# Long and short matmuls take turns on one piece of weights in a two-layer hybrid block

## The chip, the cores and the metric

One core of a Trainium2 chip runs the whole program. The metric is device microseconds of one execution. Engines: TensorE (PE; PEld is its row of weight loads), VectorE (DVE), ScalarE (ACT), GpSimd (POOL) and SyncE (SP), which issues most DMAs. TensorE's clock has two levels, 1.2 and 2.4 GHz; the profile gives the granted share.

## The reference, cut to what matters

Two layers act on 512 latent tokens and 256 context tokens of width 2048, all in float32.

```python
for l in range(2):
    sh, sc, g = split(silu(c) @ w_mod[l] + b_mod[l], 3)        # one set for latents, one for context
    hl, hc = xl * (1 + sc_l) + sh_l, xc * (1 + sc_c) + sh_c
    parts_l = split(hl @ w_in[l])       # conv u,b,c,g | q,k,v,gate | pool u,g
    parts_c = split(hc @ w_in[l])       # in the last layer only k and v
    att = softmax(q1 k1) - lam * softmax(q2 k2), applied to v   # 8 heads, keys of context and latents
    out = concat([short_conv, rms(att) * silu(gate), pool]) @ w_out[l]
    xl = layernorm(ALPHA * xl + g * out)   # and xc likewise, but in the last layer
```

What the change touches is the product `h @ w_in` for all columns but v, for both kinds of tokens at once.

## The kernel before, in words

**Numbers.** Each float32 operand is held as two halves, high and low, in a format that TensorE takes at full width (`F32R`). A product is three matmuls that accumulate in PSUM: high x high, high x low, low x high (`mm3`). The latents lie as `hhl[k]` (high) and `hll[k]` (low), 128 features by 512 tokens for each of 16 pieces k; the context as `hhc[k]` and `hlc[k]`, 128 by 256, in the tiles `hc`.

**Weights.** `WStream` brings pieces of 128 x 512 from HBM (SyncE's queue, tile `raw`), ScalarE copies the high half (`wh`, L174) and VectorE subtracts to get the low one (`wl`), up to four pieces ahead. `W.get()` hands out the next piece, `W.done()` frees its buffers for a later split.

**Stages.** A startup computes modulation and the first feature-major products; then v is made with tokens on the partitions (`v_phase`); then comes the stage of this case, 44 feature-major tiles for each layer (`mtile`); then the output product and layernorm (`gemm2`).

**`mtile`.** One call makes 128 output features for all tokens. The weights are the stationary operand (128 x 128), the tokens move past them. The sum of the latents, 512 columns, is built in one of two PSUM buffers `lat`, that of the context, 256 columns, in one of two `cps`. The loop runs over s = 0 to 7; each repetition covers two pieces k of the 16. Context tokens take part in all 44 tiles of layer 0 and in the 8 tiles of K in layer 1, 52 tiles in all; in the other 36 only the latents' matmuls run.

**Order.** All engines work through their own instruction streams, whose order the program fixes (`tc.manual_schedule()`). Attention of a head is a generator: each `step(att)` issues its next few matmuls, exponentials, transposes or subtractions between the matmuls of the tiles. With context one step stands inside a repetition (two if two heads are open) and one in `pump()` at its end. `pump` also runs work that was put off by `later` (rotary, splits of Q and K) and modulation work that is let in by a running comparison of planned VectorE and TensorE time. At s == 7 `evac` queues the copies that empty both PSUM sums, before the repetition's `pump`.

Each `PE.matmul` is recorded in the profile under the line of the wrapper that counts planned time (L53), so its rows are told apart by tiles: `lat<-hhl,wh` moves the high half of the latents past the high half of the weights, `cps<-hc,wl` the context past the low half.

Of the kernel before, what the change touches and what calls it, by code (L numbers as in the profile page):

```python
# [17 lines left out]
P = 128  # L18
D = 2048
KT = D // P  # L20
# [57 lines left out]
def body(tc, A, out):  # L78
    nc = tc.nc
    V, PE = Timed(nc.vector, dve_cost), Timed(nc.tensor, pe_cost)  # L80
    S, G, SP = nc.scalar, nc.gpsimd, nc.sync

    with tc.tile_pool(name="sb", bufs=1) as sb, tc.tile_pool(
# [115 lines left out]
        att = deque()  # L199
        modq = deque()  # L200

        def step(q):
            while q:
                try:
                    next(q[0])
                    return True
                except StopIteration:
                    q.popleft()
            return False
# [11 lines left out]
        def pump(n=1):  # L221
            for _ in range(n):
                slotn[0] += 1
                for fn in due.pop(slotn[0], ()):
                    fn()
                step(att)

                V.t = max(V.t, PE.t - LAG)
                credit[0] = min(credit[0] + rate[0], 3.0)
                if modq and credit[0] >= 1 and V.t < PE.t - left[0]:  # L230
                    credit[0] -= 1
                    step(modq)
# [62 lines left out]
        for l in range(2):  # L295
# [5 lines left out]
            for ch in range(4):  # L301
# [3 lines left out]
                for n_, k_ in enumerate(so):  # L305
                    wseq.append(A["wo"][l, ch, k_])
                    if l and n_ % 2 and (ch, n_ // 2) in SIDE:
                        extra.add(len(wseq))
                        i = SIDE.index((ch, n_ // 2))
# [13 lines left out]
        def mm3(o, hi, lo, rhi, rlo, first, last):  # L323
            PE.matmul(o, lhsT=hi, rhs=rhi, start=first, stop=False)
            PE.matmul(o, lhsT=hi, rhs=rlo, start=False, stop=False)
            PE.matmul(o, lhsT=lo, rhs=rhi, start=False, stop=last)
# [417 lines left out]
        def mtile(l, m, ctx, hook=None):  # L744
            lb[0] += 1
            pl = lat[lb[0] % 2]
            pc = cps[lb[0] % 2][:, 0:C]
            for s in range(8):
                if s % 2 == 0:
                    wh, wl = W.get()  # L750
                for hs, ps in ((hl_, pl), (hc_, pc))[:2 if ctx else 1]:
                    if hs is hc_:
                        step(att)
                        if len(att) > 1:
                            step(att)
                    for kk in range(2):
                        if not ctx and kk and len(att) > 1:
                            step(att)
                        k = 2 * s + kk
                        c = slice((k % 4) * P, (k % 4) * P + P)  # L760
                        mm3(ps, wh[:, c], wl[:, c], hs[0][k], hs[1][k], k == 0, k == KT - 1)
                if s % 2:
                    W.done()
                if s == 7:
                    evac(l, m, pl, pc)
                if hook:
                    hook(s)
                pump()

        hl_ = (hhl, hll)  # L770
        hc_ = (hhc, hlc)
# [202 lines left out]
        def evac(l, m, pl, pc):  # L974
            if M_Q <= m < M_K:
                ev_q(l, m - M_Q, pl, pc)
            elif M_K <= m < M_AG:
                ev_k(l, m - M_K, pl, pc)
            else:
                ev_x(l, m, pl, pc)  # L980
# [230 lines left out]
        for l in range(2):  # L1211
            ctx = l == 0
# [11 lines left out]
            else:  # L1224

                for k in range(KT):
                    step(hq)
                    wh, wl = W.get()
                    for i in range(4):
                        c = slice(i * P, i * P + P)  # L1230
# [30 lines left out]
            for c in lt[l]:  # L1261
                for m in c:
                    isk = M_K <= m < M_AG
                    mtile(l, m, ctx or isk, ylh if m == lt[l][-1][-1] else None)
# [79 lines left out]
```

## Time and profile before

| | |
|---|---|
| median of 3 runs | 2425.74 us (2421.2 to 2425.74) |
| the profiled execution's own time | 2427.58 us |
| its span, first to last instruction | 2425.8 us |
| TensorE busy / its loads of weights | 98% / 84% of the span |
| VectorE, ScalarE, GpSimd busy | 70%, 38%, 5% |
| mean granted clock of TensorE | 0.994 |

Busy times of TensorE come from ends that are modelled: matmuls overlap, and one that is recorded with 398 ns may be followed by the next after less. Starts are observed. A share of the whole span mixes stages, so the rows below are taken from the stage of `mtile` where that matters.

### The profile page before, as it was taken

The numbers are of one execution on the slowest core, as the hardware profiler recorded it, in microseconds if no ns is written. First come the engines' busy times: TensorE is split into PE (matmuls) and PEld (weight loads), VectorE is DVE, ScalarE is ACT, GpSimd is POOL, SyncE is SP. The second block draws the span as 40 slices with busy tenths as digits, with TensorE's granted clock in tenths as the row PEclk, the third lists the DMA queues.
The fourth block names the chain that finished last, engine by engine and source line by source line (L and its number), as shares of the span: only waits on it lengthen the run. The fifth ranks groups of instructions, "written<-read, shape, count | busy, mean of one in ns | idle before, by whom it ended". The sixth has DMA issues, their size and how long they took to land. (4 is left out here: it accounts for less than half of the span.)

```text
span 2425.8 us, 33840 instructions
## 1 busy us (share of the span) xinstructions
PE 2382.0 (98%) x12501; PEld 2032.9 (84%) x12501; DVE 1694.6 (70%) x3268; ACT 925.9 (38%) x1676; POOL 123.1 (5%) x199
## 2 busy tenths in 40 slices
PE   8999999999999999999999999999999999999997
PEld 7887888888888888888878778888888888888886
DVE  8894777787777778765486663246777677666666
ACT  4552434344343434433211153134444444444330
POOL 0000000000000000001100000000000000001102
PEclk9999999999999999999999999999999999999998
DMA  9886634343443434334456542353444434433653
GB/s 339 314 298 201 211 113 119 104 128 99 131 112 109 122 108 130 94 97 154 159 163 185 158 139 81 113 174 110 125 129 117 124 108 132 126 88 118 203 156 139
DMA packets 182169, 353.65 MB, mean 146 GB/s; under 512 B 19217, under 2 KB 43937, under 8 KB 181234
## 3 DMA queue, kind: packets, MB, share of 16 engines
q1 hardware_dynamic: 144946, 293.88, 38.8%
q0 software_dynamic: 36912, 57.55, 8.5%
q8 instruction: 98, 1.61, 0.3%
q14 instruction: 69, 0.57, 0.1%
q10 hardware_dynamic: 144, 0.05, 0.0%
HBM read 319.89 MB, written 31.51 MB: 145 GB/s over the span
## 5 line engine op out<-in xcount | busy, mean ns | idle before, releaser
L53 DVE TENSOR_TENSOR wl<-raw,wh 128x512 fp32r<-128x512 f32 x566 | 383.4, 688 | 347.8 <-ACT wh L174 346.7
L53 PE MATMUL lat<-hhl,wh 128*128 128x512 f32 x1472 | 585.6, 398 | 2.6 <-DVE Q L53 2.6
L174 ACT CAST wh<-raw 128x512 fp32r<-128x512 f32 x566 | 346.1, 619 | 614.3 <-PE SS L53 297.6
L53 PE MATMUL lat<-hll,wh 128*128 128x512 f32 x1472 | 576.6, 392 | 0.1
L53 PE MATMUL lat<-hhl,wl 128*128 128x512 f32 x1472 | 575.3, 391 | 0.0
L53 PEld LDWEIGHTS lat<-hhl,wl 128*128 128x128 f32 x1472 | 276.8, 188 | 59.6
L53 PE MATMUL cps<-hc,wh 128*128 128x256 f32 x1664 | 317.6, 284 | 0.2 <-ACT o L687 0.2
L53 PEld LDWEIGHTS lat<-hhl,wh 128*128 128x128 f32 x1472 | 277.3, 188 | 43.5 <-DVE Q L53 3.0
L53 PEld LDWEIGHTS lat<-hll,wh 128*128 128x128 f32 x1472 | 277.8, 189 | 39.7 <-DVE hll L53 0.4
L53 PEld LDWEIGHTS cps<-hc,wh 128*128 128x128 f32 x1664 | 276.7, 189 | 26.0 <-ACT o L687 0.6
L631 ACT ACTIVATE pp<-SS,smt 128x768 f32<-128x768 f32 (+1 forms) x160 | 130.9, 818 | 381.5 <-DVE smt L53 373.1
L53 PE MATMUL cps<-hc,wl 128*128 128x256 f32 x832 | 233.3, 280 | 0.0
L53 DVE CUSTOM_DVE_ANT_0 jk<-m,acc 128x512 bf16<-128x512 f32 x224 | 166.8, 745 | 19.1 <-DMA m<-in_wmbg_dram 15.2
L53 PE MATMUL SS<-wh,hc 128*128 128x512 f32 x512 | 171.1, 392 | 1.7 <-DVE aT L53 1.2
L53 PEld LDWEIGHTS cps<-hc,wl 128*128 128x128 f32 x832 | 158.9, 191 | 0.0
L53 PE MATMUL lat<-wl,hhl 128*128 128x512 f32 x364 | 144.3, 396 | 8.7 <-DVE wl L53 8.6
L53 PE MATMUL lat<-wh,hhl 128*128 128x512 f32 x364 | 145.7, 400 | 0.5 <-DVE o L53 0.5
L53 PE MATMUL lat<-wh,hll 128*128 128x512 f32 x364 | 143.6, 394 | 0.0
L53 DVE TENSOR_REDUCE smt<-SS 128x1 f32<-128x768 f32 (+1 forms) x160 | 134.9, 844 | 8.3 <-PE SS L53 7.8
L53 DVE CUSTOM_DVE_ANT_0 pp<-cv,acc 128x512 bf16<-128x512 f32 x112 | 79.8, 747 | 54.2 <-DMA cv<-in_wmbg_dram 39.3
L53 PEld LDWEIGHTS SS<-wh,hc 128*128 128x128 f32 x512 | 96.5, 188 | 24.9 <-DVE aT L53 2.1
L53 PE MATMUL SS<-K,Q 128*128 128x256 f32 (+1 forms) x432 | 109.4, 331 | 0.7 <-DVE aT L53 0.7
(269 smaller groups left out, 3552.1 us busy)
## 6 DMA issues: line engine op xcount, KB each, us to landing
raw<-in_wa_dram SPq DMA_DIRECT2D x352, 256.0 KB, 2.7
m<-in_wmbg_dram SPq DMA_DIRECT2D x200, 256.0 KB, 2.7
raw<-in_wo_dram SPq DMA_DIRECT2D x128, 256.0 KB, 3.1
wb<-in_wm0b_dram SPq DMA_DIRECT2D x32, 704.0 KB, 6.9
raw<-in_wv_dram SPq DMA_DIRECT2D x64, 256.0 KB, 3.3
cv<-in_wmbg_dram SPq DMA_DIRECT2D x56, 256.0 KB, 2.8
cv<-in_xT_dram SPq DMA_DIRECT2D x32, 384.0 KB, 4.9
v<-vsc POOLq DMA_DIRECT2D x32, 384.0 KB, 6.4
```

The source lines that it names most:

```text
L53: return fn(*a, **k)
L174: S.copy(out=h, in_=r)
L631: S.activation(out=po, in_=sv, func=AF.Exp, bias=sm[:, i:i + 1], scale=1.0, accum_out=sm[:, 2 + i:3 + i])
```

## The change

In `mtile` the two loops change places. Before, one repetition runs the latents' three matmuls for both pieces k, then attention's step, then the context's three for both pieces. After, for each piece k the three products (weights high x tokens high, high x low, low x high) are the outer loop and latents and context the inner one, so that a matmul of 512 columns and one of 256 follow each other on the same 128 x 128 piece of weights. Attention's step then stands between the two pieces k. Tiles without context keep their order.

```diff
             for s in range(8):
                 if s % 2 == 0:
                     wh, wl = W.get()
-                for hs, ps in ((hl_, pl), (hc_, pc))[:2 if ctx else 1]:
-                    if hs is hc_:
+                for kk in range(2):
+                    if kk and ctx:
                         step(att)
-                        if len(att) > 1:
-                            step(att)
-                    for kk in range(2):
-                        if not ctx and kk and len(att) > 1:
-                            step(att)
-                        k = 2 * s + kk
-                        c = slice((k % 4) * P, (k % 4) * P + P)
-                        mm3(ps, wh[:, c], wl[:, c], hs[0][k], hs[1][k], k == 0, k == KT - 1)
+                    if kk and len(att) > 1:
+                        step(att)
+                    k = 2 * s + kk
+                    c = slice((k % 4) * P, (k % 4) * P + P)
+                    first, last = k == 0, k == KT - 1
+
+                    for j, (w, i) in enumerate(((wh, 0), (wh, 1), (wl, 0))):
+                        for hs, ps in ((hl_, pl), (hc_, pc))[:2 if ctx else 1]:
+                            PE.matmul(ps, lhsT=w[:, c], rhs=hs[i][k], start=first and j == 0, stop=last and j == 2)
                 if s % 2:
                     W.done()
                 if s == 7:
```

## Rows read from the trace of the kernel before

**Rows 1.** The page: its span, and busy time of each engine.
```profile
span 2425.8 us, 33840 instructions
PE 2382.0 (98%) x12501; PEld 2032.9 (84%) x12501; DVE 1694.6 (70%) x3268; ACT 925.9 (38%) x1676; POOL 123.1 (5%) x199
```

**Rows 2.** Busy time by stage: window, length, engines' busy us, then granted clock, DMA share.
```profile
258.00:1129.00 871.00, 865.09 (x5150) 763.36 (x5149) 665.86 (x1396) 344.48 (x656) 28.92 (x44) 1.00 0.42 120
...
1594.00:2231.00 637.00, 636.00 (x3267) 541.10 (x3266) 440.48 (x781) 286.10 (x503) 25.75 (x39) 1.00 0.43 123
```

**Rows 3.** TensorE's waits, 258 to 1129 us: total, times, longest.
```profile
PE SS L53 <- ACT pp L631: 2.3, 4, 0.9
PE cps L53 <- DVE aT L53: 1.8, 2, 0.9
PE cps L53 <- DVE o L53: 1.0, 1, 1.0
```

**Rows 4.** The page's costliest groups: count, busy us, mean ns, idle before.
```profile
L53 PE MATMUL cps<-hc,wh 128*128 128x256 f32 x1664 | 317.6, 284 | 0.2 <-ACT o L687 0.2
...
L53 PEld LDWEIGHTS lat<-hll,wh 128*128 128x128 f32 x1472 | 277.8, 189 | 39.7 <-DVE hll L53 0.4
L53 PEld LDWEIGHTS cps<-hc,wh 128*128 128x128 f32 x1664 | 276.7, 189 | 26.0 <-ACT o L687 0.6
...
L53 PE MATMUL cps<-hc,wl 128*128 128x256 f32 x832 | 233.3, 280 | 0.0
```

**Rows 5.** Timeline of TensorE in layer 1, no attention: start, duration, what.
```profile
1604.45 0.39 PE L53 MATMUL lat<-hhl,wh 128*128 128x512 f32 x1
...
1605.81 0.40 PE L53 MATMUL cps<-hc,wh 128*128 128x256 f32 x2
1606.04 0.28 PE L53 MATMUL cps<-hc,wl 128*128 128x256 f32 x1
...
1606.39 0.28 PE L53 MATMUL cps<-hc,wl 128*128 128x256 f32 x1
1606.51 0.39 PE L53 MATMUL lat<-hhl,wh 128*128 128x512 f32 x1
...
1607.87 0.40 PE L53 MATMUL cps<-hc,wh 128*128 128x256 f32 x2
1608.11 0.28 PE L53 MATMUL cps<-hc,wl 128*128 128x256 f32 x1
...
1620.98 0.39 PE L53 MATMUL lat<-hhl,wh 128*128 128x512 f32 x1
```

**Rows 6.** Timeline of TensorE in layer 0, one repetition after a disturbance.
```profile
701.35 0.39 PE L53 MATMUL lat<-hhl,wh 128*128 128x512 f32 x1
...
702.04 0.39 PE L53 MATMUL lat<-hhl,wh 128*128 128x512 f32 x1
...
703.43 0.39 PE L53 MATMUL lat<-hhl,wh 128*128 128x512 f32 x1
```

**Rows 7.** Timeline of TensorE, the short matmuls of one score.
```profile
306.83 0.28 PE L53 MATMUL SS<-K,Q 128*128 128x256 f32 x1
306.94 0.28 PE L53 MATMUL SS<-v,Q 128*128 128x256 f32 x1
307.06 0.40 PE L53 MATMUL cps<-hc,wh 128*128 128x256 f32 x2
```

**Rows 8.** Timeline of TensorE, attention's product with v.
```profile
341.22 2.31 PE L53 MATMUL cps<-aT,v 128*128 128x256 f32 x18
343.37 0.41 PE L53 MATMUL cps<-hc,wh 128*128 128x256 f32 x2
```

**Rows 9.** Timeline of ScalarE at the end of a tile of K, layer 0.
```profile
291.44 0.59 ACT L819 COPY rq<-lat 128x512 f32<-128x512 f32 x1 [2.97 <-PE lat L53]
292.10 0.37 ACT L819 COPY rq<-cps 128x256 f32<-128x256 f32 x1
```

## The prediction

> **What bounds the kernel now.** I read the page first: the profiled execution spans 2425.8 us and TensorE is busy for 98% of it, VectorE for 70%, ScalarE for 38% [rows 1]. That busy time is modelled, so it says only that TensorE is the suspect. Then busy time by stage: in the feature-major products of layer 0 (258 to 1129 us) TensorE covers 865 of 871 us and in those of layer 1 (1594 to 2231 us) 636 of 637 us, at a granted clock of 1.00, the upper of its two levels, 2.4 GHz [rows 2]. Then the waits of TensorE in the longer stage: the three longest kinds sum to 2.3 + 1.8 + 1.0 = 5.1 us [rows 3]. So in both stages the queue of matmuls sets the end. A gain has to come out of the spacing of matmuls, not out of a wait.
>
> For spacing, the duration in the grouped rows (398 ns, 284 ns) is of no use, since matmuls overlap; I take start to start from the timeline. In a stretch of layer 1 without attention, eight repetitions of the loop over s (each two pieces of k: six matmuls of 512 columns and six of 256) run from 1604.45 to 1620.98 us: 16.53 / 8 = 2.066 us each, or 0.3444 us for one long and one short matmul [rows 5]. Within the first repetition the six long ones take 1605.81 - 1604.45 = 1.36 us, 0.227 each, and the six short ones 1606.51 - 1605.81 = 0.70 us, 0.117 each.
>
> **The change, part by part.** No matmul is added or removed. The edit covers 1664 + 832 = 2496 short matmuls and as many long ones (52 tiles of 48) [rows 4]. It changes three things.
>
> *Loads of weights.* The profile has one load for each matmul: 1664 loads for 1664 short matmuls of the high part. A repeat of the same piece is loaded again today: the long matmul with the low half of the latents comes right behind the one with the high half, on the same weights, and has its own 1472 loads [rows 4]. So I cost "the same piece twice in a row" at no load saved.
>
> *Spacing.* Today there are five long-to-long, one long-to-short, five short-to-short and one short-to-long step in twelve; afterwards six long-to-short and six short-to-long. The trace has both kinds. A long one followed by a short one: 1605.81 follows the last long one by the same 0.227. A short one followed by a long one: 1606.39 to 1606.51, 0.12. What the trace lacks is a short one with long ones on both sides, so this is bounded. The nearest row is the first of the short run, which has a long one before it: two short spacings in 1606.04 - 1605.81 = 0.23 us and 1608.11 - 1607.87 = 0.24 us, so 0.1175 [rows 5]. The low bound is the spacing of a score's two short matmuls behind two long ones, all four on one piece of Q: 306.83 to 306.94, about 0.1135 (half of 0.227 too), while the next, on new weights, takes 306.94 to 307.06, 0.12 [rows 7]. The high bound is attention's run on v: 18 in 343.37 - 341.22 = 2.15 us, 0.1194 each [rows 8]. I take 0.118, nearest to the rows of this very loop. A pair then costs 0.227 + 0.118 = 0.345 us against 0.3444: 0.0006 x 2496 = +1.5 us. With the low bound it is 0.0039 x 2496 = 9.7 us less, with the high one 0.0020 x 2496 = 5.0 us more.
>
> A second spacing also occurs in the loop: after some disturbances three long ones follow the short run at 0.23, from 701.35 to 702.04 (0.69 / 3), and that repetition takes 2.08 us instead of 2.066 [rows 6]. If such stretches vanished everywhere the most to win is 0.014 x 416 = 5.8 us; I take a third, 2 us less. If instead every long one behind a short one took about 0.232, the loss is 0.005 x 2496 = 12.5 us. That is the upper end.
>
> *Order around it.* Attention's step moves from behind six long ones to behind three long and three short: its two steps now stand 1.03 us apart each, where they stood 1.36 and 0.70. The number of steps, and every ScalarE, VectorE and queue instruction, stays in its order, as do the DMAs, whose issues hang on pieces of weights being split and freed. A step to the next-but-one is 2.07 us as before. Odd distances gain or lose 0.33 us; TensorE's whole wait for attention is the few us of rows 3, so I put zero there, with 3 us either way as the bound, about the 4.1 us of its two longest rows.
>
> The last long matmul of a tile now starts only 0.345 us before the tile's end instead of 0.70 + 0.227. So the copy of the latents' sum, which ScalarE was standing ready for (291.44 us, 0.59 us long, 2.97 us of idle time before it), starts 0.58 us later, and the context's copy, which ran at 292.10, queues behind it: the pair ends some 0.5 us later [rows 9]. Queued behind them on ScalarE are the split of the next weights and attention's exponentials. What hides it: the next tile uses the other PSUM buffer, a later step consumes the copies one to four repetitions on, and ScalarE is busy for only 344 of 871 us [rows 2]. Where that cover is gone, at the end of layer 0, TensorE already waits 1.0 us for VectorE's gate [rows 3]: I add 0.5 us. Uncovered for all 52 tiles it would be 26 us, which the near-absence of waits makes unlikely.
>
> Sum: +1.5 - 2 + 0.5 = 0.0 us on the profiled execution's own 2427.58 us (1.8 us more than its span). The runs shown have a median of 2425.74, 1.84 below that execution, so I state 2426.
>
> **A rule against this reading.** The rows say that a repeated piece is loaded again and that a long matmul is spaced 0.227 whether or not its weights repeat [rows 4, 5]. The Trainium skill (TensorE: Matmul & The Clock Gate, Part 2, step 1) says that weights are loaded apart from the matmul so that one load can serve several. By that the second load of each pair would be saved; the 1472 repeated loads disagree. The same page (Part 1, "Wait — 56ns, not 53.3ns?") gives 215.7 ns between 512-column matmuls at the upper clock; if missing loads brought the long ones there, the sum would be 2496 x 0.011 = 28 us less, 2398, as an estimate from that page. No run here shows it.
>
> **The rivals.** *Faster, the short matmul stops waiting for a load.* If the load of one piece can be skipped or run ahead because the piece repeats, each short spacing falls to 0.1135: for it speak the four score matmuls on one Q [rows 7]; against it, that the first two of the short run share their weights as well and take 0.1175 [rows 5]. Worked out: 2426 - 9.7 - 1.5 = 2415. Chance 0.17.
>
> *Slower, the long one behind a short one keeps the upset spacing.* Place: every short-to-long step, now 2496 instead of 416. For it: rows 6, where exactly the long ones behind a short run are late. Against: rows 5, where they aren't. At 0.232 each it gives 2426 + 12.5 = 2438. It decides from 0.002 us per pair on (4.9 us). Chance 0.16.
>
> *Slower, the late copies.* ScalarE's half microsecond per tile reaches TensorE through the exponentials; it takes more than ten of the 52 tiles exposed to show. Half of them: 2426 + 13 = 2439. Against it speaks the idle time ahead of those copies. Chance 0.05.
>
> *No effect at all*, since spacing depends only on the columns of the matmul in front: that is the forecast, 0.62.
>
> **How the numbers follow.** A difference of 0.2% (4.9 us) is about what a measurement of this kernel can tell from none. The likeliest case holds 2421 to 2431; the first rival lies about 2415, the other two about 2438. With the bounds of the short spacing and the run-to-run spread (2421.2 to 2425.74) the range is 2414 to 2439. Faster 0.17, same 0.62, slower 0.16 + 0.05 = 0.21.
>
> **What will show it.** Counts first: 1664 and 832 short matmuls, each with its load; fewer loads would make the first rival. In a stretch without attention a repetition should read 2.06 to 2.08 us, alternating 0.227 and 0.118. A repetition of 2.04 says first rival, 2.10 second. TensorE's waits in the first stage should stay below 10 us; more, on the scores or the transposes, says late copies. I am wrong if the alternation of operands and PSUM banks at every matmul has a price of its own, of which the trace before shows nothing.

## The result, and the profile after

| | before | after |
|---|---|---|
| median of 5 runs each, us | 2424.0 (2421.2 to 2425.74) | 2449.83 (2445.29 to 2450.7) |
| ratio, 95% interval | | 1.01 [1.0086, 1.0114] |
| span of the profiled execution, us | 2425.8 | 2448.0 |

The change costs 1.0%, 24 us (20.9 to 27.6 by the interval). The forecast was no change, 2426, with 2439 as the upper end. All figures below in "us against before" are the ratio less one, times 2425, with the interval worked out in the same way, so that runs of different chips can be set side by side.

Where the loss lies is seen first from busy time by stage, with the window moved to the same matmuls in each kernel: from the stage's first long matmul to the first matmul that follows its tiles (that of attention's normalization in layer 0, that of the output product in layer 1). Window, length, busy us of TensorE, its loads, VectorE, ScalarE and GpSimd, then granted clock and DMA. Of the kernel before:

```profile
257.12:1128.47 871.35, 865.44 (x5151) 763.76 (x5151) 665.87 (x1397) 344.26 (x656) 28.92 (x44) 1.00 0.42 120
1593.57:2232.96 639.39, 637.84 (x3275) 542.35 (x3273) 441.59 (x784) 287.68 (x506) 25.85 (x40) 1.00 0.43 123
```

Of the kernel after:

```profile
257.13:1149.16 892.03, 877.41 (x5150) 770.88 (x5150) 665.55 (x1397) 340.86 (x656) 28.68 (x44) 1.00 0.41 118
1613.37:2256.01 642.64, 639.75 (x3275) 543.43 (x3273) 441.42 (x784) 286.85 (x506) 25.60 (x40) 1.00 0.42 123
```

Layer 0, where 44 tiles have context, is 20.7 us longer, layer 1, where 8 have, 3.3 us; the rest of the program is not longer. The clock is the same. In layer 0 TensorE's busy time rises by 12.0 us, so 20.7 - 12.0 = 8.7 us are idle time on top: two kinds of loss, one in spacing and one in waits.

Spacing, from the timeline of the kernel after in a stretch without attention (start, duration, what):

```profile
270.31 0.40 PE L53 MATMUL lat<-hhl,wh 128*128 128x512 f32 x1
270.55 0.28 PE L53 MATMUL cps<-hc,wh 128*128 128x256 f32 x1
270.67 0.39 PE L53 MATMUL lat<-hll,wh 128*128 128x512 f32 x1
270.90 0.28 PE L53 MATMUL cps<-hc,wh 128*128 128x256 f32 x1
271.01 0.40 PE L53 MATMUL lat<-hhl,wl 128*128 128x512 f32 x1
...
271.71 0.40 PE L53 MATMUL lat<-hll,wh 128*128 128x512 f32 x1
```

Against [rows 5]: short ones still take 0.12 (270.55 to 270.67, 270.90 to 271.01), long ones take 0.24 and 0.23 by turns (270.31 to 270.55, 270.67 to 270.90), and the pattern repeats every two pairs: 271.01 - 270.31 = 271.71 - 271.01 = 0.70 us, 0.350 a pair instead of 0.3444.

That is a clean stretch. Over the whole stage of layer 0 (from 264 us on, starts of all matmuls of the loop that have matmuls of the loop on both sides, waits left out) a pair takes 345.7 ns before in the mean and 350.3 after, a long matmul 228.5 and 232.6. The kernel before has upset stretches too: a fifth of its long spacings are over 231 ns, against half after. The difference of 4.6 ns makes 11.5 us for 2496 pairs.

Waits of TensorE in the stage of layer 0 (total, times, longest), after:

```profile
PE cps L53 <- DVE aT L53: 4.1, 2, 2.1
PE SS L53 <- ACT pp L631: 3.9, 5, 1.4
PE cps L53 <- ACT o L687: 3.3, 4, 1.2
...
PE SS L53 <- DVE aT L53: 1.7, 1, 1.7
```

Against [rows 3] the wait for attention's weights aT has gone from 1.8 to 4.1 us and the one for the exponentials (pp) from 2.3 to 3.9; the third row is all but new. It says exactly what waits: the context's sum (`cps`) waits for ScalarE's o, that is, the first short matmul of a tile waits until ScalarE has read attention's product out of the other half of the same PSUM buffer (a copy, then its square, L687). It was 0.2 us before:

```profile
PE cps L53 <- ACT o L687: 0.2, 1, 0.2
```

And ScalarE at the end of a tile of K, after:

```profile
292.50 0.59 ACT L820 COPY rq<-lat 128x512 f32<-128x512 f32 x1 [3.86 <-PE lat L53]
292.98 0.38 ACT L820 COPY rq<-cps 128x256 f32<-128x256 f32 x1
293.24 0.63 ACT L174 CAST wh<-raw 128x512 fp32r<-128x512 f32 x1
```

The idle time ahead of the copy is 3.86 us instead of 2.97 [rows 9]: the copy of the latents' sum waits longer for TensorE, and what is queued on ScalarE behind it, or on VectorE for its result, can be late with it.

### The profile page after: what moved, and what is told of

It is laid out like the page before. It is cut to its first block, busy times and chain, and to the rows that moved or that the text cites. A ratio compares the mean times of both kernels' runs of the same rounds, so it can differ in the third digit from the quotient of the medians.

```text
span 2448.0 us, 33840 instructions
## 1 busy us (share of the span) xinstructions
PE 2393.7 (98%) x12501; PEld 2039.2 (83%) x12501; DVE 1694.6 (69%) x3268; ACT 921.5 (38%) x1676; POOL 122.5 (5%) x199
## 4 chain that ended last, share of the span: by engine, by line
PE 61%; DVE 6%; DMA 4%; issue 2%; ACT 1%; DVEq 0%; SPq 0%; ACTq 0%
PE lat L53 37%; PE cps L53 13%; PE SS L53 11%; DMA cv<-in_wmbg_dram 3%; DVE pp L53 2%; DVE wl L53 1%; DVE z L53 1%; DMA cv<-srow 1%; DVE bst L53 0%; DMA raw<-in_wo_dram 0%; DVE smt L53 0%; DMA m<-in_wmbg_dram 0%; DVE o L53 0%; DVE jk L53 0%; ACT wh L174 0%
## 5 line engine op out<-in xcount | busy, mean ns | idle before, releaser
L53 PE MATMUL lat<-hhl,wh 128*128 128x512 f32 x1472 | 594.0, 404 | 2.1 <-DVE Q L53 2.1
L53 PE MATMUL cps<-hc,wh 128*128 128x256 f32 x1664 | 467.8, 281 | 4.3 <-ACT o L687 4.3
L53 PEld LDWEIGHTS cps<-hc,wh 128*128 128x128 f32 x1664 | 316.7, 190 | 8.2 <-ACT o L687 6.2
```

What stands on the lines that cost most here:

```text
L53: return fn(*a, **k)
```

## The experiments

The theory after the result: three losses. (a) Spacing: a long matmul behind a single short one is spaced 6 ns more in the mean. (b) The last long matmul of a tile is late, and with it ScalarE's and VectorE's copies and attention. (c) The first short matmul of a tile is early and meets the copy out of its PSUM buffer. The rival: all is spacing.

**First repetition in the old order.** `if ctx and s == 0:` the loop of before, `else:` the new one.

> Only the first repetition (s = 0) of each tile with context runs in the old order: six long matmuls, attention's step, six short ones; the other seven take turns. Theory A (about half of the loss is waits, and the largest new one is the first short matmul of a tile, which now stands 0.23 us behind the tile's start instead of 1.36 us and waits for ScalarE's copy of attention's product out of the same PSUM buffer): that wait, 4.3 us in all after the change, goes back to 0.2, the time falls by 4 to 7 us to about 2444, one eighth of the spacing loss (1.3 us) among it. Rival B (all of the loss is spacing): only 2 to 3 us less, an eighth of 25.

Measured: 2442.89, ratio 1.0071 [1.0059, 1.0084], 17.2 us against before, so about 7 us less than after. The wait of cps on ScalarE's copy fell from 3.3 to 0.6 us in the stage of layer 0, the one on aT stayed (4.2). Loss (c) is there.

**Attention's step later.**

```diff
-                    if kk and ctx:
-                        step(att)
 ...
                     for j, (w, i) in enumerate(((wh, 0), (wh, 1), (wl, 0))):
+                        if kk and ctx and j == 1:
+                            step(att)
 ...
```

> The matmuls take turns as after the change, but attention's step stands behind the fourth of the six pairs (1.38 us into a repetition, as the 1.36 us of before) instead of the third. Theory A with waits from the moved step: the waits of attention's transposes, scores and products on ScalarE and VectorE (12 us after, 6.7 before) fall by 3 to 5 us and the time with them. Rival B (spacing alone), and the rival that the new waits come from the late copies: no change beyond 2 us.

Measured: 2447.18, 1.0086 [1.0072, 1.01], 20.9 us. Its interval overlaps that of after, so the moved step is not shown to cost; 3 us is the most likely size. The waits on aT (4.1 in the whole span) and on the copy (4.2) stayed, so neither comes from the step's place in the middle of a repetition alone.

**Last repetition in the old order.** As the first run, with `s == 7`.

> Only the last repetition (s = 7) of each tile with context runs in the old order, so that the latents' sum is complete 0.7 us before the tile's end again and ScalarE's copies start as early as before. Theory C (late copies carry the waits): 5 to 8 us less than after the change. Theories A and B: one eighth of the spacing loss, 1.3 to 3 us less.

Measured: 2438.4, 1.0051 [1.0037, 1.0065], 12.4 us, so 12 us less than after, more than expected. In the stage of layer 0 the wait on aT is back at 1.7 us, on pp at 2.3, on the copy at 1.9.

**The last, and the first, repetition alone in the new order**, all else as before (`if not (ctx and s == 7):` the old loop; and the same with `s == 0`).

> The kernel before, with only the last repetition (s = 7) of each tile with context in the new order. Theory C (the latents' sum is complete 0.58 us later, so ScalarE's and VectorE's copies, and all that is queued behind them, are late): 6 to 11 us more than before, 2431 to 2436, and more waits of TensorE on ScalarE and VectorE. Spacing alone: one eighth of 10 us, 1 to 2 us more.

> The kernel before, with only the first repetition (s = 0) of each tile with context in the new order, so that the first short matmul of a tile stands 0.23 us behind the tile's start instead of 1.36. If it then waits for the copy of attention's product out of the same PSUM buffer, TensorE shows some 4 us of waits on ScalarE's copies out of cps and the time is 4 to 7 us above before, 2430 to 2433. If that wait only arose because ScalarE was late from the tile's end, little shows: 2425 to 2428.

Measured: the last alone 2433.48, 1.0035 [1.0022, 1.0048], 8.5 us; the first alone 2429.9, 1.0017 [1.0008, 1.0027], 4.1 us. Waits of TensorE in the stage of layer 0, last repetition alone:

```profile
PE SS L53 <- ACT pp L631: 5.0, 5, 2.1
PE cps L53 <- DVE aT L53: 4.2, 2, 2.1
...
PE cps L53 <- ACT o L687: 0.6, 1, 0.6
```

First repetition alone:

```profile
PE SS L53 <- ACT pp L631: 2.0, 4, 0.8
PE cps L53 <- ACT o L687: 1.9, 3, 0.8
PE cps L53 <- DVE aT L53: 1.7, 2, 0.8
```

Each part brings its own kind of wait and hardly the other's: the late end of the long ones brings those on pp and aT, the early first short one that on the copy: 1.9 us, and 2.9 in the whole span, where some 4 were expected. The pp rows compare less well: the longest wait of the last alone stands at 318 us, soon behind the start of the stage, and from 257 to 265 us the granted clock was 1.00 in that run and 0.79 in the profile of before.

The wait on aT is the sharpest sign. In all runs whose last repetition has the old order it is 1.6 to 1.8 us, in all whose last repetition takes turns 4.1 to 4.2, and its two places in the program are the same ones at which the kernel before waits. How it grows can be followed at the first of them, in timelines of the three engines. Before:

```profile
567.78 0.82 PE L53 MATMUL SS<-ident,pp 128*128 128x128 f32 x6
567.99 0.60 ACT L800 ACTIVATE rq<-lat 128x512 f32<-128x512 f32 x1 [1.42 <-PE lat L53]
568.62 0.75 DVE L53 STREAM_SHUFFLE cv<-rq 128x512 f32<-128x512 f32 x1
573.67 0.95 DVE L53 TENSOR_TENSOR aT<-SS,aT 128x768 fp32r<-128x768 f32 x1
574.67 1.57 PE L53 MATMUL cps<-aT,v 128*128 128x256 f32 x11 [0.89 <-DVE aT L53]
```

Last repetition alone in the new order:

```profile
566.99 0.82 PE L53 MATMUL SS<-ident,pp 128*128 128x128 f32 x6
568.76 0.60 ACT L814 ACTIVATE rq<-lat 128x512 f32<-128x512 f32 x1 [2.68 <-PE lat L53]
569.40 0.75 DVE L53 STREAM_SHUFFLE cv<-rq 128x512 f32<-128x512 f32 x1
574.45 0.95 DVE L53 TENSOR_TENSOR aT<-SS,aT 128x768 fp32r<-128x768 f32 x1
575.46 1.82 PE L53 MATMUL cps<-aT,v 128*128 128x256 f32 x7 [2.11 <-DVE aT L53]
```

In this last repetition attention's step issues six transposes (first row). Before, they stand behind all six long matmuls; now they stand in front of the last three. The last long matmul starts 568.34 - 565.95 = 2.39 us into the repetition, before 567.55 - 566.42 = 1.13: 1.26 us later, where it is 0.60 us later in last repetitions without matmuls of a step. A step's matmuls lie in the last repetition of 11 of the 44 tiles of layer 0; in eight of them the last long one is 1.26 to 1.34 us later. The copy rq starts 1.77 us behind the transposes instead of 0.21. VectorE's rotary work begins with that copy, and the subtraction that completes aT is queued on VectorE 5.05 us behind the rotary's start in both. TensorE waits 2.11 us instead of 0.89. The delay went through VectorE's queue; no exponential of ScalarE lies on this path. For the waits put down to pp the path was not followed.

**Both ends old, turns between** (`s in (0, 7)` in the old order).

> First and last repetition of each tile with context in the old order, the six between take turns as after the change. If the three parts add, what is left is six eighths of the spacing loss of about 10 us: 2432 to 2435, with TensorE's waits as before. If the waits came back without the early first short matmul and the late last long one, they belong to taking turns itself: 2437 or more.

Measured: 2430.88, 1.0029 [1.0018, 1.0039], 7.0 us. Waits in the same stage:

```profile
PE cps L53 <- DVE aT L53: 1.6, 2, 0.8
PE SS L53 <- ACT pp L631: 1.5, 2, 0.9
...
PE cps L53 <- ACT o L687: 0.2, 1, 0.2
```

All three kinds are at or below their size of before, so what is left belongs to spacing: 7.0 us for six of the eight repetitions, 9.3 for eight (5.8 to 12.6 by the interval). The mean pair of the stage, 348.8 ns against 345.7, makes 7.7 us.

**Threes.** For each k three long, then three short matmuls (`mm3` for latents, then for context). **Twos.** Two long, two short, over the six products of a repetition. **Other weights.** Turns as after, but the short matmul of a pair takes the other k:

```diff
-                    k = 2 * s + kk
 ...
                         for hs, ps in ((hl_, pl), (hc_, pc))[:2 if ctx else 1]:
+                            k = 2 * s + (1 - kk if hs is hc_ else kk)
+                            c = slice((k % 4) * P, (k % 4) * P + P)
```

> For each piece k three long matmuls and then three short ones: the step and the first short matmul stand nearly as after the change, but there are two changes from short to long in twelve matmuls instead of six (before: one). Theory S1 (each long matmul that has a short one before it costs 6 ns more, 0.233 on average instead of 0.227): a repetition without attention takes 2.066 + 2 x 0.006 = 2.08 us, against 2.10 after the change, and the time falls by about 7 us, to 2443. Rival S2 (the price is in any mixing of long and short inside one piece k): spacing as after the change, 2.10 us.

> Two long and two short matmuls take turns (three changes from short to long in twelve). If what costs is a single short matmul alone between long ones, a repetition without attention takes 2.066 us as with threes, and the time is near that of threes, 2435 to 2440. If each change from short to long costs something and threes only happened to stay below it, a repetition takes 2.08 us or more and the time is 2441 to 2446.

> Long and short matmuls take turns as after the change, but the two of a pair use different pieces of weights (the short one that of the other k). Theory S1 (a single short matmul between two long ones costs, whatever its weights): long spacings alternate between 0.227 and 0.239 as after the change, a repetition without attention takes 2.10 us, the time is that of after, 2447 to 2452. Rival S3 (the same piece loaded twice in a row costs): 2.07 us, and 8 to 12 us less, about 2440.

Measured: threes 2436.7, 1.0045 [1.0033, 1.0058], 10.9 us; twos 2443.39, 1.0072 [1.0059, 1.0084], 17.5 us; other weights 2449.66, 1.0098 [1.0082, 1.0113], 23.8 us. These runs also move the first short and the last long matmul, so their spacing is read from timelines without attention. Threes, four groups of six matmuls:

```profile
263.83 0.39 PE L53 MATMUL lat<-hhl,wh 128*128 128x512 f32 x1
...
267.96 0.39 PE L53 MATMUL lat<-hhl,wh 128*128 128x512 f32 x1
```

4.13 / 12 pairs = 0.344, as before, which neither theory expected. Twos, one repetition:

```profile
265.90 0.39 PE L53 MATMUL lat<-hhl,wl 128*128 128x512 f32 x1
...
268.00 0.39 PE L53 MATMUL lat<-hhl,wl 128*128 128x512 f32 x1
```

2.10 / 6 = 0.350, as after: my theory that only a single short one costs falls. Over the whole stage threes are not free, though: their mean pair is 348.0 ns, that of twos 350.2, against 345.7 before and 350.3 after. With one, two, three and six changes from short to long in twelve matmuls the price rises up to three and then no more, so a fixed price per change falls too. Other weights, four pairs:

```profile
263.86 0.40 PE L53 MATMUL lat<-hhl,wh 128*128 128x512 f32 x1
...
265.26 0.40 PE L53 MATMUL lat<-hll,wh 128*128 128x512 f32 x1
```

1.40 / 4 = 0.350 again, and 350.3 ns over the stage: that a pair shares its piece of weights neither gains nor costs anything that these runs can tell.

**Three stretches by themselves.** In the tile Q of head 0, layer 0, the short matmul moves 512 columns; in the tile K of that head both move 256; in the tile Q of layer 1 the latents' matmuls go into `lat` and `cps` by turns:

```python
PE.matmul(cps[lb[0] % 2], lhsT=w[:, c], rhs=hca[i][:, 2 * s:2 * s + 2].rearrange("p a b -> p (a b)"), ...)
...
PE.matmul(ps, lhsT=w[:, c], rhs=hs[i][k][:, 0:C], ...)
...
PE.matmul((pl, cps[lb[0] % 2])[n % 2], lhsT=w[:, c], rhs=hl_[i][k], ...)
```

> Three stretches without attention measure spacing by themselves; their results are changed, so only spacing is read. Tile Q of head 0, layer 0: the short matmul moves 512 columns of context (two pieces) instead of 256. Tile K of head 0, layer 0: both move 256 columns (half of the latents left out). Tile Q of head 0, layer 1: latents alone, with even and odd matmuls into two PSUM banks. If mixing lengths is what costs, the first reads 0.227 for every matmul, the second 0.117 to 0.118, the third 0.227. If taking turns between two PSUM banks costs, all three read more, 0.233 in the mean for 512 columns. If taking turns between two moving tensors costs, the first reads 0.233 and the third 0.227.

One run; it computes something else than the reference, so only spacing is read. Timeline, the three stretches in this order:

```profile
264.56 0.39 PE L53 MATMUL lat<-hhl,wh 128*128 128x512 f32 x1
264.79 0.39 PE L53 MATMUL cps<-hc,wh 128*128 128x512 f32 x1
...
265.92 0.39 PE L53 MATMUL lat<-hhl,wh 128*128 128x512 f32 x1
...
282.28 0.28 PE L53 MATMUL lat<-hhl,wh 128*128 128x256 f32 x1
...
283.68 0.28 PE L53 MATMUL lat<-hhl,wh 128*128 128x256 f32 x1
...
1613.01 0.39 PE L53 MATMUL lat<-hhl,wh 128*128 128x512 f32 x1
1613.24 0.39 PE L53 MATMUL cps<-hll,wh 128*128 128x512 f32 x1
...
1617.09 0.39 PE L53 MATMUL lat<-hhl,wh 128*128 128x512 f32 x1
```

Six in 1.36 us are 0.227 each, twelve in 1.40 are 0.117, eighteen in 4.08 are 0.227. With equal lengths neither the turns between two moving tensors nor those between two PSUM buffers cost anything. What is left is the mixture of lengths.

**Threes with both ends old.** First and last repetition in the old order, threes between.

> First and last repetition of each tile with context in the old order, the six between in threes. If the parts add (the wait of the first short matmul, the late copies, the spacing of single short ones) nothing of the loss is left: 2424 to 2430. If something else in the changed order costs, 2432 or more.

Measured: 2430.99, 1.002 [1.0011, 1.0029], 4.9 us: a bit outside what I expected, and not to be told from turns between the same ends (7.0). Threes are at 0.344 in clean stretches, but the mean pair over this run's stage is 347.4 ns against 345.7, which makes 4.2 us: the loss that stays with them is spacing as well.

**The long ones ahead.** The latents' six matmuls run one repetition ahead of the context's (in the last, the context's twelve follow); the second run also moves attention's step in the first and last repetition.

> The opposite of the change's side effects on the old order: the latents' six long matmuls run one repetition ahead of the context's six short ones, so that the latents' sum is complete 1.4 us before the tile's end (before: 0.7) and the first short matmul of a tile stands 2.7 us behind its start (before: 1.36). If late copies and the early first short one are what waits come from, the waits of before (some 7 us on attention) shrink and the time is 2 to 5 us below before, 2420 to 2424. If the waits of before have other causes, 2424 to 2428; if the longer hold on the weights' buffers matters, more.

> As the run with the long matmuls one repetition ahead, but attention's step is put into the middle of the six long ones in the first repetition and behind nine of eighteen in the last, so that no two steps stand with nothing between them. If the 18 us of that run came from steps too close together, most of it goes: 2424 to 2432, and under 2424 if an early latents' sum also helps. If it came from holding the weights longer or from the order itself, it stays at 2438 or more.

Measured: 2444.76, 1.0078 [1.0064, 1.0092], 18.9 us, and 2442.03, 1.0073 [1.006, 1.0086], 17.7 us. In both the outcome is the one that was named for the case that the longer hold on the weights, or the order itself, costs. An early sum alone wins nothing, and the steps' distance in two repetitions isn't the reason. TensorE's longest waits in the stage of layer 0, first of the two:

```profile
PE SS L53 <- ACT pp L631: 9.6, 9, 2.5
PE SS L53 <- DVE aT L53: 3.7, 3, 3.2
```

So here too attention is late. This order holds each piece of weights for one repetition more, which may delay the splits on ScalarE and VectorE; whether that is the cause was not separated. So the cause of this loss stays open. No version that was run beats the kernel before.

## Why the prediction was wrong

**That TensorE's queue bounds both stages**: right; the loss appeared in them and nowhere else.

**No load of weights saved**: right. 12501 loads for 12501 matmuls before and after, and the run with other weights has the time of after. The rival that a repeated piece lets the short one run sooner is out: short spacing stayed at 0.117 to 0.118.

**Spacing, "a pair then costs 0.227 + 0.118 = 0.345"**: the short term was right, the long one failed. I took the spacing of a long matmul with a long one before it for that of a long one with a short one on either side, and bounded only the short one with care. Measured is 0.350 a pair in a clean stretch. The second rival (0.232 for each long one, chance 0.16) had the size, 232.6 ns in the mean, but not the place: by its rule every long one behind a short one is late, and the rows show 0.24 and 0.23 by turns; twos, with half as many such steps, cost the same. That it came so near is in part luck. The loss is (0.350 - 0.3444) x 2496 = 14 us by clean stretches, 11.5 by the means of the stage, and 9.3 by the run with both ends old. The 2 us that I took off for vanishing upset stretches failed as well: half of the long spacings are over 231 ns now, where a fifth were.

**Late copies, "what hides it" and "I add 0.5 us"**: failed. The last repetition alone costs 8.5 us, of which an eighth of 11.5, 1.4 us, is spacing: some 7 us where I put 0.5. Two steps were wrong. "Starts 0.58 us later" holds where no step of attention has matmuls in the last repetition (measured 0.60); where one has, three long matmuls now stand behind it, and the delay is mostly 1.26. And the cover that I named, a low share of busy time on ScalarE, was no cover: the delay went on through VectorE's queue, where rotary work waits for the copy and the subtraction for aT stands behind it; VectorE is busy for 665 of 871 us [rows 2], and my argument left it out. "The near-absence of waits" didn't speak against it either: a place that waits 0.9 us has no slack left, and there the delay of 1.2 us came through whole. The upper bound that I gave (26 us) held; the case had a chance of 0.05.

**The first short matmul**: missing from the sum. I looked at what the end of a tile releases and not at what its start waits for. In the old order six long matmuls, 1.36 us, hid the copy of attention's product out of the other half of the same PSUM buffer; in the new one 0.23 us do. Alone 4.1 us, 2.7 without its eighth of spacing; taken away from after, 7.0.

**The sum**: 11.5 + 7.1 + 2.7 = 21.3 us, against 24.2 (20.9 to 27.6). The parts are larger when taken out of after (12 for the last, 7 for the first) than when put into before (8.5 and 4.1), by some 3 us each. They may reinforce each other, but each of these differences is of the size of its interval, so that isn't shown.

**The moved step at zero, with 3 us as the bound**: not contradicted where the step was moved by itself. What I missed is that in the last repetition its matmuls now stand in front of the latents' last three.

## What to carry to other kernels

When the order of matmuls changes inside a stage that TensorE bounds, ask of every PSUM buffer both when its last matmul comes (what of other work now stands in front of it, who copies it, and what is queued behind the copy, on every engine that uses the result) and when its first one comes (what still has to be read out of it): a microsecond of matmuls in front of a buffer's first use can be the only thing that hides the copy that empties it. Spacing of matmuls of one length can't be carried over to a mixture of lengths; it has to be measured in that very pattern. A stretch of a few microseconds without other work shows the pattern, but the mean over the stage gives the price: threes look free in the one, and in the other they have half of the spacing loss of the turns. Two matmuls on the same piece of weights, one behind the other, gained nothing here, where every matmul had its own load (12501 of each).

## What the hardware showed that I had not expected

At a granted clock of 1.00 and in clean stretches a long matmul (512 columns) and a short one (256) cost 0.3444 us in groups of three or six, but 0.350 in groups of one or two; over the stage the means are 345.7 ns (six), 348.0 (three), 350.2 (two) and 350.3 (one). With equal lengths, one by one, there is no such extra. Nor is there in the one stretch at the lower clock that was read, at the start of the stage in the kernel after (first row: busy time and granted clock, 0.50):

```profile
258.60:261.80 3.20, 3.20 (x12) 2.72 (x11) 2.07 (x8) 2.38 (x6) 0.00 (x0) 0.50 0.91 289
259.32 0.63 PE L53 MATMUL lat<-hhl,wl 128*128 128x512 f32 x1
...
260.60 0.63 PE L53 MATMUL lat<-hll,wh 128*128 128x512 f32 x1
```

Two pairs take 1.28 us, 0.640 each, which is 768 columns at 1.2 GHz with nothing between. At 2.4 GHz 768 columns would be 0.320, so in clean stretches each pair holds 0.024 us more than that in groups of three or six and 0.030 in smaller ones. What that time is no run here shows.
